# Where two of five weight groups begin inside their buffers in a three-term float32r input projection

## The chip, the cores and the metric

The kernel runs on one core of one Trainium2 chip. The metric is the device time of one execution in microseconds (us). Three runs of the kernel before took 2325.15, 2329.02 and 2332.24 us; their median is 2329.02 us.

## What is computed

One layer of a streaming encoder, for a prompt of 2048 tokens and for 8 sequences of 16 tokens (together 17 tiles of 128 tokens, width 1024). The part that the change touches is the first matrix product:

```python
def trunk_layer(x, ...):
    qm, km, vm, om, ip, fp, qa, ka, va = split_in(x @ w_in)
    ...                                    # mLSTM over chunks, sliding-window attention
    mix = jnp.concatenate([hm, ha], axis=-1) @ w_out
    h = layer_norm(DEEPNORM_ALPHA * x + mix, ln1_g, ln1_b)
    f, conv_rows = conv_ffn(h, conv_prev, w_up, w_conv, b_conv, w_down)
    y = layer_norm(DEEPNORM_ALPHA * h + f, ln2_g, ln2_b)
```

`x @ w_in` is called the in-projection here. It is followed by the output projection (`w_out`), the up-projection (`w_up`, 5632 columns) and the down-projection (`w_down`).

## The kernel before

**Arithmetic.** Every operand of a large product is split into a high part, rounded to float32r by a ScalarE copy, and a low part, the VectorE difference (`split`, lines 218 to 221). A product is then three matmuls: high by high, high by low, low by high.

**In-projection.** The 17 tiles stand in four blocks (`IBLOCKS`): five tiles, then three times four. The columns of `w_in` stand in five groups of 512, `g` = 0 to 4: groups 0 and 1 hold the mLSTM queries and keys, 2 the attention queries, 3 the output gate, 4 the values. Gates and attention keys and values are a sixth, narrower product (`i_direct`, line 760). Each block and group is a 2x2 block product done with seven products instead of eight (`s` = 1 to 7), on sums of quarters. One product (`i_product`, lines 722 to 746) is 24 matmuls at line 735, each with a stationary operand of 128x128 and a moving operand of 128x256: four output quarters, two steps `k`, three terms. The last of the five tiles of block 0 is multiplied apart at line 744.

Which operand is stationary depends on the group:

```python
l, r = (w[:, k, m], x[:, k]) if g < 2 else (x[:, k, m], w[:, k])
mm(o, l, r, ...)
```

In groups 0 and 1 the weights are loaded into the array and the tokens stream past; in groups 2, 3 and 4 it is the other way round. At line 744 the tokens are stationary and the weights move, in every group.

**Where the operands lie.** A weight unit (one product's weights, 1024 float32 in each of 128 partitions, high and low) takes two buffers from `half` (line 396), which hands out the tags `wlo` and `whi` in turn, four buffers each. A buffer is 4608 bytes per partition, since the gate weights (`[P, 2, 2, 288]`, line 485) use the same tags. In the built program the eight buffers begin at 3072, 7680, 12288, 16896, 37888, 42496, 47104 and 51712 bytes into the partition, all multiples of 512. The token operands `oh` and `ol` (`x_slot`, line 543) lie 4096 bytes apart from 65088 on, so each begins 64 bytes after a multiple of 512; that comes from the 256 unused bytes that `self.skew(self.xp, 256)` puts ahead of them (line 246). Within a tile the operands of line 735 begin at multiples of 512 bytes. So before the change the weights begin at 0 and the tokens at 64, counted modulo 512. The token operands of line 744 begin at 384 or 480.

The later projections have other pairs. In the output projection (lines 225 to 227) tokens at 64 are stationary and weights at 0 move, 512 columns at a time. In the up-projection (line 1878; weights stationary, 384 or 320 columns move) and the down-projection (line 2082; tokens stationary, 512 columns move) both operands begin at 0.

**Order.** TensorE's instructions run in the order in which they are written out; the in-projection's products are woven with the chains of the mLSTM and the attention (`Chains.weave`). Weight units are loaded and split ahead as buffers come free (`advance`, `next_raw`, `next_split`). For groups 0 and 1 every weight unit is split by lines 220 and 221 (in blocks 1 to 3 too); only units of groups 2, 3 and 4 are also kept in memory after the split and loaded back by DMA (`kept`, line 425; lines 493 and 533).

Of the kernel before, what the change touches and what calls it, by code (L numbers as in the profile page):

```python
# [14 lines left out]
P = 128  # L15
# [189 lines left out]
class Prog:  # L205
# [269 lines left out]
    def next_split(self):  # L475
        V = self.nc.vector
        if self.us >= self.ur:
            return False
        u = self.uq[self.us]
        need = 1 if u[0] == "g" else 2  # L480
        if self.halves[0] - self.halves[1] + need > self.ring:
            return False
        self.us += 1
        if u[0] == "g":
            e = self.raw_of.pop(u)
            w = self.half([P, 2, 2, 288])[:, :, :, :264]
            self.split(w[:, 0], w[:, 1], e[0])
            e[1] = True
            self.wu[u] = w[:, 0], w[:, 1]
            return True  # L490
        hi, lo = self.half([P, 1024]), self.half([P, 1024])
        if self.kept(u):
            for i, t in enumerate((hi, lo)):
                self.nc.sync.dma_start(t.bitcast(F32), self.zws[u[2]][SUMS.index(u[3])][i].rearrange("p a b -> p (a b)"))
        elif u[0] == "p" and u[1] == 0:
            self.split_first(u[2], u[3], hi, lo)
        else:
            e = self.raw_of.pop(u)
            self.split(hi, lo, e[0].rearrange("p a b -> p (a b)"))
            e[1] = True  # L500
        v = lambda t: t.rearrange("p (a b) -> p a b", a=2 if u[0] == "o" else 4)
        self.wu[u] = v(hi), v(lo)
        return True
# [1670 lines left out]
```

## Time and profile before

| | before |
|---|---|
| median of three runs | 2329.02 us |
| time of the profiled execution | 2327.77 us |
| its span, first to last instruction | 2325.5 us |
| TensorE, matmuls busy | 2292.0 us (99%) |
| TensorE, weight loads busy | 2113.6 us (91%) |
| VectorE busy | 1803.0 us (78%) |
| ScalarE busy | 1305.4 us (56%) |
| mean granted TensorE clock | 0.996 |

The trace gives each matmul a start and a length. The ends are modelled, and the lengths (276 ns and more at line 735) overlap, because the next matmul starts before the one ahead has left the array. So what a stream of matmuls costs is read from the distance of their starts, here called the pace, and not from their length. A row of the timeline merges neighbours of one form: `x2` is two matmuls, and the start shown is that of the first. PE is TensorE's matmuls, PEld its weight loads, DVE VectorE, ACT ScalarE.

### The profile page before, as it was taken

How to read it: one execution, taken by the hardware profiler on the slowest of the kernel's cores; microseconds unless marked ns; L12 is line 12 of the kernel's file. 1: busy time of each engine (PE TensorE's matmuls, PEld its weight loads, DVE VectorE, ACT ScalarE, POOL GpSimd, SP SyncE). 2: the span in 40 equal slices, each digit the busy share in tenths (PEclk: the TensorE clock that was granted, in tenths of full speed). 3: DMA queues.
4: the chain of work that ended last, by engine and by line, in shares of the span. 5: the costliest groups of instructions: out<-in, count | busy, mean ns of one | idle time of the engine just before them, and what ended most of it. 6: DMA issues, size and time to landing. Idle time of an engine off the chain costs nothing.

```text
span 2325.5 us, 39932 instructions
## 1 busy us (share of the span) xinstructions
PE 2292.0 (99%) x14425; PEld 2113.6 (91%) x14425; DVE 1803.0 (78%) x3150; ACT 1305.4 (56%) x2465; POOL 238.0 (10%) x298
## 2 busy tenths in 40 slices
PE   9989999999999999999999999999999999999998
PEld 8989998999987777999999999999999988888887
DVE  8676586787778888987888766778766787796897
ACT  5353466676665665655556455556555644554653
POOL 0101101101111221300002000001000000000100
PEclk9999999999999999999999999999999999999999
DMA  8888889889977667787777899988998886766753
GB/s 281 276 311 283 284 285 315 292 279 341 305 250 262 208 222 242 258 321 286 286 270 251 277 314 327 307 306 268 324 297 265 248 284 224 243 198 215 243 192 109
DMA packets 297365, 624.98 MB, mean 269 GB/s; under 512 B 47052, under 2 KB 140240, under 8 KB 297168
## 3 DMA queue, kind: packets, MB, share of 16 engines
q1 hardware_dynamic: 296304, 619.29, 78.2%
q10 hardware_dynamic: 864, 3.15, 0.4%
q8 instruction: 114, 1.87, 0.3%
q14 instruction: 83, 0.68, 0.1%
HBM read 451.78 MB, written 170.56 MB: 268 GB/s over the span
## 4 chain that ended last, share of the span: by engine, by line
PE 73%; DVE 6%; issue 2%; DMA 2%; ACT 2%; POOL 0%; SPq 0%; DVEq 0%; ACTq 0%; POOLq 0%
PE dps L1878 18%; PE fup L1878 18%; PE dps L2082 6%; PE dps L735 6%; PE fht L2082 5%; PE fup L2082 5%; PE dps L225 2%; PE dps L227 2%; PE dps L226 2%; PE ppo L1371 1%; PE psc L1322 1%; PE ppt L1365 1%; PE dps L760 1%; DVE uw L221 1%; DVE w L221 1%
## 5 line engine op out<-in xcount | busy, mean ns | idle before, releaser
L1878 PE MATMUL dps<-hh,uw 128*128 128x384 f32 (+1 forms) x1848 | 477.5, 327 | 5.3 <-DVE u L1911 2.6
L1878 PE MATMUL fup<-hh,uw 128*128 128x384 f32 (+1 forms) x1848 | 476.4, 326 | 0.0
L1926 DVE SCALAR_TENSOR_TENSOR cc<-u,cw,cc 128x768 f32<-128x768 f32 (+1 forms) x264 | 257.6, 977 | 124.5 <-ACT cc L1924 121.0
L1878 PEld LDWEIGHTS dps<-hh,uw 128*128 128x128 f32 x1848 | 329.2, 188 | 7.6 <-DVE u L1911 3.2
L1878 PEld LDWEIGHTS fup<-hh,uw 128*128 128x128 f32 x1848 | 329.2, 188 | 0.0
L1878 PE MATMUL fup<-hl,uw 128*128 128x384 f32 (+1 forms) x924 | 301.3, 326 | 0.6 <-DVE hl L221 0.6
L1878 PE MATMUL dps<-hl,uw 128*128 128x384 f32 (+1 forms) x924 | 301.0, 326 | 0.0
L735 PE MATMUL dps<-w,oh 128*128 128x256 f32 x1344 | 255.0, 285 | 5.3 <-ACT zev L801 3.6
L221 DVE TENSOR_TENSOR w<-wraw,w 128x1024 fp32r<-128x1024 f32 (+2 forms) x163 | 188.1, 1159 | 60.8 <-ACT w L220 59.5
L220 ACT CAST w<-wraw 128x1024 fp32r<-128x1024 f32 (+2 forms) x163 | 161.0, 993 | 122.0 <-PE dps L735 58.2
L735 PEld LDWEIGHTS dps<-w,oh 128*128 128x128 f32 x1344 | 212.5, 191 | 17.7 <-issue 8.9
L220 ACT CAST uw<-wraw 128x1024 fp32r<-128x1024 f32 x126 | 123.2, 981 | 173.3 <-PE dps L2082 104.1
L221 DVE TENSOR_TENSOR uw<-wraw,uw 128x1024 fp32r<-128x1024 f32 x126 | 142.4, 1130 | 64.0 <-ACT uw L220 63.8
L735 PE MATMUL dps<-w,ol 128*128 128x256 f32 x672 | 188.3, 280 | 0.0
L1924 ACT ACTIVATE cc<-u,cw 128x768 f32<-128x768 f32 (+1 forms) x132 | 132.0, 1000 | 95.3 <-DVE u L1920 92.4
L735 PE MATMUL dps<-oh,w 128*128 128x256 f32 x896 | 171.2, 284 | 5.6 <-ACT zev L801 1.6
L1878 PEld LDWEIGHTS fup<-hl,uw 128*128 128x128 f32 x924 | 173.5, 188 | 1.4 <-DVE hl L221 1.4
L1878 PEld LDWEIGHTS dps<-hl,uw 128*128 128x128 f32 x924 | 173.5, 188 | 0.0
L2082 PE MATMUL fup<-uw,fu 128*128 128x512 f32 x726 | 169.1, 389 | 0.0
L2082 PEld LDWEIGHTS fup<-uw,fu 128*128 128x128 f32 x726 | 136.2, 188 | 28.3 <-ACT fht L2089 0.2
L2082 PE MATMUL dps<-uw,fu 128*128 128x512 f32 x660 | 160.9, 389 | 0.1
L735 PEld LDWEIGHTS dps<-oh,w 128*128 128x128 f32 x896 | 140.8, 188 | 12.3 <-issue 4.1
(337 smaller groups left out, 4612.5 us busy)
## 6 DMA issues: line engine op xcount, KB each, us to landing
uw<-zw SPq DMA_DIRECT2D x176, 512.0 KB, 5.1
zw<-uw SPq DMA_DIRECT2D x88, 512.0 KB, 2.8
w<-zws SPq DMA_DIRECT2D x72, 512.0 KB, 6.6
wv<-wup SPq DMA_DIRECT2D x66, 512.0 KB, 5.9
wraw<-wi SPq DMA_DIRECT2D x64, 512.0 KB, 5.1
wraw<-zt SPq DMA_DIRECT2D x60, 512.0 KB, 4.2
wraw<-wdn SPq DMA_DIRECT2D x45, 512.0 KB, 3.7
wraw<-wo SPq DMA_DIRECT2D x40, 512.0 KB, 4.6
```

What stands on the lines that cost most here:

```text
L220: nc.scalar.copy(hi, src)
L221: nc.vector.tensor_sub(lo, src, hi.bitcast(F32))
L225: mm(out, ah, bh, start=start, stop=False)
L226: mm(out, ah, bl, start=False, stop=False)
L227: mm(out, al, bh, start=False, stop=stop)
L735: mm(o, l, r, start=s in (1, 7) and c == k == i == 0, stop=k == 3 and i == 2, skip_group_check=True)
L760: mm(o, x, w, start=k == i == 0, stop=k == KD - 1 and i == 2, skip_group_check=True)
L1322: nc.tensor.matmul(ps[kvh][:, j, :nk], q[rs, j0 + j], k[rs, sel], start=i == 0, stop=i == 2)
L1878: mm(ps, l[:, k], r[:, k], start=s in (1, 7) and k == 0 and i == 0, stop=k == 3 and i == 2, skip_group_check=True)
L1924: S.activation(c[:, v], u[:, v, 2:2 + n], AF.Identity, bias=w[3], scale=w[2])
L1926: V.scalar_tensor_tensor(c[:, v], u[:, v, i:i + n], w[i], c[:, v], op0=ALU.mult, op1=ALU.add)
L2082: mm(ps, l[:, k, c], r[:, k], start=s in (1, 4, 7) and u == 0 and k == 0 and i == 0, stop=u == nu - 1 and k == n - 1 and i == 2, skip_grou ...
```

## The change

The high and low buffers of a weight unit of groups 0 and 1 (`u[0] == "p" and u[2] < 2`) are taken 128 float32 wider, and the unit's 1024 numbers are put 16 numbers (64 bytes) into them. All other units, those of the output projection among them, stay as they are.

```diff
-        hi, lo = self.half([P, 1024]), self.half([P, 1024])
+        at = 16 if u[0] == "p" and u[2] < 2 else 0
+        hi, lo = [self.half([P, 1024 + 8 * at])[:, at:at + 1024] for _ in range(2)]
```

The wider tile is 4608 bytes, the size that the buffer has already: in the built program every tile begins at the same address as before, and each engine has the same instructions in the same order with the same waits. What differs is the address inside the buffer at which ScalarE and VectorE write the split weights of groups 0 and 1 and at which TensorE reads them. They begin at 64 modulo 512 now, as the tokens do.

## The prediction

> **What bounds the kernel now.** I read the page's head and its busy times first, then the busy time by stage, the groups that use the weight tiles, and the timeline of TensorE in stretches without other work.
>
> ```profile
> span 2325.5 us, 39932 instructions
> PE 2292.0 (99%) x14425; PEld 2113.6 (91%) x14425; DVE 1803.0 (78%) x3150; ACT 1305.4 (56%) x2465; POOL 238.0 (10%) x298
> PE 73%; DVE 6%; issue 2%; DMA 2%; ACT 2%; POOL 0%; SPq 0%; DVEq 0%; ACTq 0%; POOLq 0%
> ```
>
> TensorE has a matmul in flight for 99% of the span, and 73% of the chain that ended last is its own. So nearly every nanosecond that is put between two matmuls should arrive in the total. The stages confirm it where the change lies (span, then PE, PEld, DVE, ACT, POOL busy, granted clock, DMA share, GB/s):
>
> ```profile
> 0.00:70.00 70.00, 64.51 (x505) 62.46 (x506) 58.02 (x104) 37.55 (x60) 0.31 (x5) 1.00 0.83 281
> 70.00:650.00 580.00, 567.69 (x4722) 534.74 (x4722) 414.81 (x1001) 341.56 (x786) 70.79 (x58) 0.99 0.87 297
> ```
>
> From 70 to 650 us TensorE is idle for 12.3 us of 580. In the first 70 us it is idle for 5.5.
>
> **How many matmuls are touched.** The groups of line 735 that read a weight tile, and line 744 beside them:
>
> ```profile
> L735 PE MATMUL dps<-w,oh x1344: 276/276/582, 70.1 to 640.7; 128*128 128x256 f32 x192
> L735 PE MATMUL dps<-oh,w x896: 276/279/471, 6.0 to 552.5; 128*128 128x256 f32 x180
> L735 PE MATMUL dps<-ol,w x448: 276/279/415, 6.2 to 552.4; 128*128 128x256 f32 x150
> L744 PE MATMUL psx<-w,xs x240: 274/280/415, 11.3 to 156.8; 128*128 128x256 f32 x120
> ```
>
> The moving operand's name stands first. Tokens move past weights (`oh,w` and `ol,w`) in 896 + 448 = 1344 matmuls; these are groups 0 and 1, and their stationary operand shifts by 64 bytes. The 2016 with the weights moving (`w,oh`, and `w,ol` in the same proportion) are groups 2 to 4 and keep their addresses.
>
> **What one costs now.** Starts in a clean stretch of group 0 in block 1, weights stationary:
>
> ```profile
> 184.97 0.40 PE L735 MATMUL dps<-oh,w 128*128 128x256 f32 x2
> ...
> 187.79 0.40 PE L735 MATMUL dps<-oh,w 128*128 128x256 f32 x2
> ```
>
> Between these two rows lie 24 matmuls: 2.82 us / 24 = 117.5 ns. The same form in a stretch of group 3, tokens stationary:
>
> ```profile
> 137.77 0.39 PE L735 MATMUL dps<-w,oh 128*128 128x256 f32 x2
> ...
> 140.49 0.39 PE L735 MATMUL dps<-w,oh 128*128 128x256 f32 x2
> ```
>
> 2.72 us / 24 = 113.3 ns. The same size, the same array, the same clock, and 4.2 ns apart; what differs is which operand lies at 0 and which at 64. But the two paces are not tied to the two layouts alone. Once the weights-stationary form ran at the fast pace, and once the other ran at the slow one:
>
> ```profile
> 74.47 0.39 PE L735 MATMUL dps<-oh,w 128*128 128x256 f32 x2
> ...
> 76.51 0.39 PE L735 MATMUL dps<-oh,w 128*128 128x256 f32 x2
> ```
>
> ```profile
> 236.46 0.40 PE L735 MATMUL dps<-w,oh 128*128 128x256 f32 x2
> ...
> 238.94 0.40 PE L735 MATMUL dps<-w,oh 128*128 128x256 f32 x2
> ```
>
> 18 matmuls in 2.04 us are 113.3 ns each; 21 in 2.48 us are 118.1. So a stream falls into one of two steps and keeps it for tens of matmuls. The layout seems to decide which step is the usual one.
>
> **The change part by part.** No instruction, wait or transfer is added, removed or moved, so no queue is passed and no buffer comes free at another point of the program. Two kinds of access change their address.
>
> The writes: 56 units (14 products in 4 blocks) are cast by line 220 and subtracted by line 221, now to a place 64 past a multiple of 512. Token tiles are already written to such places, by lines 580 and 581:
>
> ```profile
> L220 ACT CAST w<-wraw 128x1024 fp32r<-128x1024 f32 x108 | 113.1, 1051 | 94.8 <-PE dps L735 51.6 <-DMA wraw<-wi 12.1 <-PE psx L744 10.8
> L580 ACT CAST oh<-xr 128x1024 fp32r<-128x1024 f32 x23 | 24.0, 1051 | 4.9 <-DVE xr L572 4.3 <-DVE xr L568 0.2 <-DMA xr<-xq 0.2
> L221 DVE TENSOR_TENSOR w<-wraw,w 128x1024 fp32r<-128x1024 f32 x108 | 133.3, 1237 | 49.7 <-ACT w L220 48.6 <-DMA zqa<-zev 0.4 <-DMA wraw<-zws 0.2
> L581 DVE TENSOR_TENSOR ol<-xr,oh 128x1024 fp32r<-128x1024 f32 x23 | 28.5, 1241 | 1.9 <-ACT oh L580 1.9
> ```
>
> 1051 against 1051 ns and 1237 against 1241: the writes cost nothing, and would cost nothing much without cover, since VectorE is busy 414.81 of 580 us there.
>
> The reads: from the pair (stationary 0, moving 64) they go to (64, 64). No 256-column row of the trace has equal places. Wider matmuls with both operands at 0 do: up-projection with 384 and 320 columns, down-projection with 512. The fourth pair is the output projection, 512 columns, stationary at 64 and moving at 0:
>
> ```profile
> 999.71 0.33 PE L1878 MATMUL dps<-hl,uw 128*128 128x384 f32 x1
> ...
> 1001.27 0.33 PE L1878 MATMUL fup<-hl,uw 128*128 128x384 f32 x1
> ```
>
> ```profile
> 1699.94 0.31 PE L1878 MATMUL fup<-hl,uw 128*128 128x320 f32 x1
> ...
> 1700.82 0.31 PE L1878 MATMUL dps<-hl,uw 128*128 128x320 f32 x1
> ```
>
> ```profile
> 2104.82 2.88 PE L2082 MATMUL fht<-uw,fu 128*128 128x512 f32 x12
> 2107.54 0.84 PE L2082 MATMUL dps<-uw,fu 128*128 128x512 f32 x3
> ```
>
> ```profile
> 672.91 0.39 PE L225 MATMUL dps<-w,oh 128*128 128x512 f32 x1
> ...
> 675.01 0.39 PE L225 MATMUL dps<-w,oh 128*128 128x512 f32 x1
> ```
>
> 9 matmuls of 384 columns take 1.56 us, 173.3 each; 6 of 320 take 0.88, 146.7; 12 of 512 take 2.72, 226.7; 9 in the output projection take 2.10, 233.3. The three with equal places lie on one line: 26.6 ns for 64 columns and 53.4 for 128 are both 0.417 ns per column, which leaves 13.3 ns above 320 x 0.417 = 133.4. Carried down to 256 columns that is 106.7 + 13.3 = 120.0 ns. It is an extrapolation: at 256 columns the two known pairs (113.3 and 117.5) lie below the line, so a matmul this short need not behave as the wide ones.
>
> Bounds: at best the shifted form takes the fast step that it has once taken already, 113.3 ns. At worst it pays the line and also what the unequal pair pays at 512 columns, 233.3 - 226.7 = 6.6, so 126.6. I take 120.0, the value from equal places; 117.5 unchanged lies close to it.
>
> Sum: 1344 x (120.0 - 117.5) = +3.4 us. Line 744 moves the shifted weights in 8 of its 20 groups of 12, 96 matmuls, with tokens at 384 or 480; at the 4.2 ns by which the paces differ that is at most 0.4 us either way, taken as 0. Of TensorE's waits in the first 650 us the longest follow its own work:
>
> ```profile
> PE dps L735 <- ACT zev L801: 5.1, 5, 2.3
> PE dps L735 <- ACT zev L793: 2.3, 2, 1.2
> ```
>
> ScalarE copies there what TensorE has just finished, so these 7.4 us move along and absorb nothing. I pass all of the sum on. The profiled execution took 2327.77 us (2.3 around its span); 2327.8 + 3.4 = 2331.2. The median of the runs shown is 1.25 us above that execution, within their spread of 7.1. I name 2331.
>
> **The rivals.** *The fast step* (30%): with the stationary operand at 64, as in groups 2 to 4, the stream settles at 113.3 ns. For it: the stretch at 74.47 us shows that weights-stationary matmuls can run so, and the usual home of that step is a stationary operand at 64. Against it: there the moving operand is at 0, not at 64. It gives 1344 x 4.2 = -5.6 us, 2322.2.
>
> *The address does not matter* (17%): the step is set by how a stream begins, and the usual step of groups 0 and 1 has another cause, such as the order of operands (the stationary one repeated, not the moving one). For it: both paces occur at both layouts. Against it: the split between the groups is too regular for chance. It gives 0, so 2327.8 to 2329. The Trainium skill has this as a rule: "SBUF — State Buffer", section "Who interferes with whom", gives TensorE two independent read ports, one for the moving operand and one for weight loads, and says that it never waits on anyone. By that rule the time stays at 2327.8; the 6.6 ns between the two 512-column streams speak against it here.
>
> *Places count one by one* (13%, the slow side): not the distance of the two operands decides but each start for itself, and a stationary start at 64 costs the 6.6 ns that it seems to cost in the output projection, on top of the line. Then 126.6 ns, 1344 x 9.1 = +12.2 us, 2340. Against it: at 256 columns the stationary start at 64 belongs to the faster group.
>
> My forecast has 38%. The last 2% are other mishaps.
>
> **How the numbers follow.** A measurement of this kernel can tell about 0.3%, 7 us, from no change. The forecast and the no-effect case lie inside that. The fast step lies at 5.6 us, and with some 2 us of scatter in a median it counts as faster in four of ten cases: 0.12, and 0.01 from the rest. Places one by one is slower nearly always, 0.12, and the forecast now and then, 0.03. That leaves 0.72 for the same. The range 2321 to 2337 holds the first three cases but for the lower third of the fast step, and leaves out the slow side: 0.10 + 0.10.
>
> **What would show it.** In the changed profile, the distance of starts in clean stretches of `oh,w`: 120.0 ns if I am right, 113.3, 117.5 or 126.6 for the rivals. Stretches of `w,oh` should stay at 113.3, lines 220 and 221 at 1051 and about 1237 ns, the three wide streams at 146.7, 173.3 and 226.7. I am wrong in kind if the pace is right and the total is not: then idle time has grown or shrunk elsewhere. I am wrong in size if the shifted stream has a third step that no row here shows.

## The result, and the profile after

| | before | after |
|---|---|---|
| median of 12 runs each | 2329.05 us | 2333.47 us |
| lowest to highest | 2325.15 to 2332.24 us | 2327.62 to 2337.48 us |
| profiled execution (its span) | 2327.77 us (2325.5) | 2337.15 us (2334.9) |
| mean granted TensorE clock in it | 0.996 | 0.994 |

The ratio is 1.0019, with a 95% interval of 1.001 to 1.0027: between 2.3 and 6.3 us slower. That is less than the 0.3% that the prediction counts as a change. It lies above the predicted 2331 and inside 2321 to 2337.

The head of the page of the kernel after, its busy times and its chain by engine:

```profile
span 2334.9 us, 39932 instructions
PE 2299.0 (98%) x14425; PEld 2120.2 (91%) x14425; DVE 1802.0 (77%) x3150; ACT 1305.2 (56%) x2465; POOL 245.2 (10%) x298
PE 74%; DVE 6%; issue 3%; DMA 3%; ACT 2%; POOL 0%; SPq 0%; DVEq 0%; POOLq 0%; ACTq 0%
```

The instruction counts are those of before, and TensorE still sets the end. Its busy time has grown by 7.0 us and VectorE's has not. What has changed is in the starts. The groups of the in-projection by operands (line 736 now; shortest, median and longest in ns, then the first and the last start) show where it lies:

```profile
L736 PE MATMUL dps<-oh,w x896: 274/283/470, 6.0 to 560.9; 128*128 128x256 f32 x180
L736 PE MATMUL dps<-w,oh x1344: 276/276/582, 72.1 to 649.6; 128*128 128x256 f32 x192
```

The modelled lengths say little (medians of 283 and 276 ns for 279 and 276), but the last matmul of groups 2 to 4 starts at 649.6 us, where it started at 640.7. So 8.9 of the 9.4 us between the spans arise before 650 us. The pace is in the timeline of a clean stretch of group 0 in block 1, the place shown of before:

```profile
185.64 0.40 PE L736 MATMUL dps<-oh,w 128*128 128x256 f32 x2
...
193.92 0.40 PE L736 MATMUL dps<-oh,w 128*128 128x256 f32 x2
```

69 matmuls in 8.28 us are 120.0 ns each, where it was 117.5 (117.8 over 69 matmuls of the same stretch). The untouched form, tokens stationary, has the pace of before: 63 matmuls in 7.14 us, 113.3 ns.

```profile
106.41 0.39 PE L736 MATMUL dps<-w,oh 128*128 128x256 f32 x2
...
113.55 0.39 PE L736 MATMUL dps<-w,oh 128*128 128x256 f32 x2
```

Nor did a wide stream move: the mean distances of starts of the 320-column, the down-projection's and the output projection's matmuls are 146.7, 226.9 and 233.1 ns in both kernels. In the up-projection 6 matmuls of 384 columns take 1.04 us, 173.3 each:

```profile
1002.56 0.33 PE L1879 MATMUL fup<-hl,uw 128*128 128x384 f32 x1
...
1003.60 0.33 PE L1879 MATMUL dps<-hl,uw 128*128 128x384 f32 x1
```

The writes to the shifted place, by shape (busy us in all, then the mean ns of one), take 1051 ns as before, and 1239 for 1237:

```profile
L220 ACT CAST w<-wraw 128x1024 fp32r<-128x1024 f32 x107 | 112.1, 1051 | 96.6 <-PE dps L736 52.9 <-DMA wraw<-wi 13.7 <-DVE wraw L519 10.9
L221 DVE TENSOR_TENSOR w<-wraw,w 128x1024 fp32r<-128x1024 f32 x107 | 132.3, 1239 | 50.5 <-ACT w L220 50.0
```

The pace accounts for 1344 x 2.5 = 3.4 us, not for the 9.4 us between the two profiled executions. The rest of that is mostly the granted clock of this one execution. Below are three stretches of the kernel before and then of the kernel after (columns as in the prediction: stretch, its length, PE, PEld, DVE, ACT, POOL busy, granted clock, DMA share, GB/s):

```profile
0.00:100.00 100.00, 94.51 (x766) 92.46 (x767) 77.71 (x124) 49.72 (x76) 2.47 (x6) 1.00 0.81 279
100.00:250.00 150.00, 143.30 (x1177) 139.55 (x1178) 102.32 (x158) 64.24 (x95) 22.56 (x16) 0.98 0.85 294
250.00:350.00 100.00, 97.52 (x813) 91.59 (x810) 70.93 (x175) 53.91 (x125) 7.55 (x7) 0.97 0.85 284
```

```profile
0.00:100.00 100.00, 94.31 (x744) 92.45 (x745) 74.24 (x120) 49.84 (x76) 2.47 (x6) 0.98 0.79 272
100.00:250.00 150.00, 141.79 (x1152) 137.97 (x1151) 103.35 (x160) 62.06 (x92) 22.57 (x16) 0.99 0.84 291
250.00:350.00 100.00, 95.93 (x790) 91.02 (x789) 66.06 (x159) 50.51 (x115) 6.57 (x6) 0.92 0.82 270
```

Multiply each stretch by what its clock lacks to 1.00: before loses 0 + 3 + 3 = 6 us, after 2 + 1.5 + 8 = 11.5. The 5.5 us between them and the pace's 3.4 make 8.9 of 9.4. (The clock column is rounded; added up dip by dip from the trace, the losses are 6.8 and 11.9 us.) From 350 to 2320 us both kernels have 1.00. So one execution can't size this change; the medians of 12 can.

### The profile page after: what moved, and what is told of

It reads as the page before. It is cut to its first block, busy times and chain, and to the rows that moved or that the text cites. A ratio compares the mean times of both kernels' runs of the same rounds, so it can differ in the third digit from the quotient of the medians.

```text
span 2334.9 us, 39932 instructions
## 1 busy us (share of the span) xinstructions
PE 2299.0 (98%) x14425; PEld 2120.2 (91%) x14425; DVE 1802.0 (77%) x3150; ACT 1305.2 (56%) x2465; POOL 245.2 (10%) x298
## 4 chain that ended last, share of the span: by engine, by line
PE 74%; DVE 6%; issue 3%; DMA 3%; ACT 2%; POOL 0%; SPq 0%; DVEq 0%; POOLq 0%; ACTq 0%
PE dps L1879 18%; PE fup L1879 18%; PE dps L736 7%; PE dps L2083 6%; PE fht L2083 5%; PE fup L2083 5%; PE dps L225 2%; PE dps L227 2%; PE dps L226 2%; PE ppo L1372 1%; PE psc L1323 1%; PE ppt L1366 1%; PE dps L761 1%; DVE w L221 1%; DMA txy<-wdn 1%
```

## Experiments

The account tested here is that the distance between the starts of the two operands sets the pace. Two others stand beside it: that each place counts for itself, and that the address has no effect. All experiments but the repetitions move operands, and all leave every instruction in its place. Their diffs are against the kernel after, or against the kernel before where its line stands behind the minus; the second line of the first one, the same width for every `at`, belongs to all that set `at` for both halves. Two figures stand for each run: the pace in a clean stretch, and the mean distance of starts over all in-projection matmuls whose successor starts within 160 ns (some 1240 with weights stationary, 1850 with tokens stationary). By that mean before has 117.6 and 114.6, after 119.7 and 114.7. "Distance" is the stationary operand's start minus the moving one's, in bytes: before -64 in groups 0 and 1, after 0. Times are medians, beside those of the kernel before on the same chip.

### Stationary operand 64 bytes past the moving one

```diff
-        at = 16 if u[0] == "p" and u[2] < 2 else 0
-        hi, lo = [self.half([P, 1024 + 8 * at])[:, at:at + 1024] for _ in range(2)]
+        at = 32 if u[0] == "p" and u[2] < 2 else 0
+        hi, lo = [self.half([P, 1152 if at else 1024])[:, at:at + 1024] for _ in range(2)]
```

> Weights of groups 0 and 1 begin 128 bytes in: stationary 128, moving 64. Theory A (the distance of the two starts decides, modulo 512): the distance is +64, as in groups 2 to 4, so the weights-stationary stream falls to 113.3 ns, 1344 x 4.2 = 5.6 us less than before, about 2323. Theory B (each start counts for itself, starts off a multiple of 512 cost): no faster than the 119.7 ns of the changed kernel, 2332 or more. Theory C (addresses have no part): 117.5 ns and the time of before, 2329.

The same units as in the change, 128 bytes into their buffers: the stationary operand at 128, the moving one at 64. The timeline:

```profile
182.30 0.39 PE L736 MATMUL dps<-oh,w 128*128 128x256 f32 x2
...
190.12 0.39 PE L736 MATMUL dps<-oh,w 128*128 128x256 f32 x2
```

69 matmuls in 7.82 us: 113.3 ns, the fast step, now usual in groups 0 and 1 too. The mean fell from 117.6 to 114.8, and 1344 x 2.8 = 3.8 us. Measured: 2326.03 against 2329.64 us, so -3.6 between the medians; the ratio is 0.9988 (0.9978 to 0.9998), a gain of 0.5 to 5.1 us. That is less than the 5.6 expected, since not every stretch ran at 113.3. Another 64 bytes in the same direction turn the loss into a gain, so it is excluded that the address doesn't matter. In the one profiled execution, though, waits took the gain: without what the clock lost up to there, its last in-projection matmul starts at 634.5 us, that of the kernel before at 633.9; the distances of 300 ns and more between starts add up to 52.8 us there, and to 48.8 before.

### A whole period further

```diff
-        at = 16 if u[0] == "p" and u[2] < 2 else 0
+        at = 128 if u[0] == "p" and u[2] < 2 else 0
```

> Weights of groups 0 and 1 begin 512 bytes in, in the same enlarged tile as in the change. Theory A with a period of 512 bytes: the pair is (0, 64) again, 117.5 ns and the time of before, 2329. If the change cost time by the larger tile or by the mere shift, or if the period is longer: another pace, or 2333 as in the changed kernel.

512 bytes on, the pair is (0, 64) again, though the offset inside a wider buffer is the largest tried. The timeline:

```profile
183.21 0.40 PE L736 MATMUL dps<-oh,w 128*128 128x256 f32 x2
...
191.33 0.40 PE L736 MATMUL dps<-oh,w 128*128 128x256 f32 x2
```

69 matmuls in 8.12 us are 117.7 ns each, and the mean is 117.5: the pace of before. The time was 2331.84 against 2329.64 us, ratio 1.0013 (1.0003 to 1.0023), an excess that no pace explains. The same program a second time:

> Weights of groups 0 and 1 begin 512 bytes in, a second time. Its pace was that of before (117.5 ns), its ratio 1.0013. Theory A: 1.000, and the first ratio was scatter between executions (the granted clock). If the larger tile or the shift itself costs time outside the matmul streams: again about 1.001.

2329.01 against 2329.82 us, 0.9994 (0.9983 to 1.0005), with a mean of 117.5 again. The excess of the first time did not come back. Two runs of the same program lie 2.8 us apart in their medians, and their intervals overlap only between 1.0003 and 1.0005. This is the caution for all totals below.

### Distance 0 in all groups

```diff
-        at = 16 if u[0] == "p" and u[2] < 2 else 0
+        at = 16 if u[0] == "p" else 0
```

> Weights of all five groups begin 64 bytes in: the pair is (64, 64) at all of line 735. Theory A: groups 2 to 4 go from 113.3 to 120.0 ns too, 2016 x 6.7 = 13.5 us on top of the 3.4 of groups 0 and 1, about 2346. Theory B with a moving start of 64 as the dear one (it is what groups 0 and 1 have and groups 2 to 4 lack): groups 2 to 4 go to 117.5, 8.5 us on top, about 2341. Theory C: no more than the changed kernel, 2333.

Now the moving weights of groups 2 to 4 begin at 64 as well, beside stationary tokens at 64:

```profile
136.12 0.40 PE L736 MATMUL dps<-w,oh 128*128 128x256 f32 x2
...
144.40 0.40 PE L736 MATMUL dps<-w,oh 128*128 128x256 f32 x2
```

69 in 8.28 us: 120.0 ns, as with the weights stationary. So it isn't the order of the operands, nor whether the stationary one is repeated. The total missed what was expected: 2336.18 against 2329.64 us, ratio 1.0026 (1.0013 to 1.004), +6.5. By the means it should have been 1344 x 2.1 + 2016 x 5.1 = 13.1, beyond the interval's 9.3. The rest is taken up by waits. TensorE's waits for ScalarE in the in-projection:

```profile
PE dps L736 <- ACT zev L794: 2.0, 2, 1.1
...
PE dps L736 <- ACT zev L802: 1.8, 3, 0.8
```

3.8 us together, where before had 7.4. A slower TensorE seems to leave ScalarE time to catch up. Those are two waits among many. Counted by starts, the distances of 300 ns and more in the in-projection (clock dips left out) add up to 42.1 us here, and to between 48.5 and 51.5 in the five profiled executions with the pace of before (before itself 48.8). So some 6 to 9 us of pauses are gone, which is what the total lacks.

### Both operands at 0

```diff
-            self.skew(self.xp, 256)
+            self.skew(self.xp, 192)
-            self.skew(wx, 448)
+            self.skew(wx, 512)
```

> The weights stay at 0 and the tokens move from 64 to 0: the pair is (0, 0) in the in-projection and in the output projection. Theory A: 120.0 ns at all of line 735 (1344 x 2.5 + 2016 x 6.7 = +16.9 us), and the output projection's 512-column stream falls from 233.3 to 226.7 (816 x 6.6 = -5.4 us): about 2340. Theory B: both operands are at the cheap place, so line 735 stays at 113.3 or below in groups 2 to 4 and falls below 117.5 in groups 0 and 1, with the output projection 5.4 us less: 2323 or below. Theory C: 2329.

The kernel before, with the tokens moved back by 64 bytes instead of the weights forward: (0, 0) in all groups, and in the output projection too. The timeline, tokens stationary and then weights stationary:

```profile
136.21 0.40 PE L735 MATMUL dps<-w,oh 128*128 128x256 f32 x2
...
144.49 0.40 PE L735 MATMUL dps<-w,oh 128*128 128x256 f32 x2
...
169.86 0.40 PE L735 MATMUL dps<-oh,w 128*128 128x256 f32 x2
...
177.78 0.40 PE L735 MATMUL dps<-oh,w 128*128 128x256 f32 x2
```

69 in 8.28 and 66 in 7.92 us, 120.0 both. (0, 0) costs what (64, 64) costs, so places do not count one by one. 2335.24 against 2329.64 us, ratio 1.0031 (1.0017 to 1.0046), +5.6, again less than expected. In the output projection, however, 512 columns at distance 0 are cheaper: a mean of 228.8 ns where before has 233.1. 816 matmuls x 4.3 would be 3.5 us, and the sum of the means, 1344 x 2.2 + 2016 x 5.2 - 3.5 = 9.9 us, lies inside the interval (4.0 to 10.7). But the trace shows the parts otherwise. From its first matmul to its last the output projection takes 284.2 us here and 284.4 before: what its stream gains is lost again in longer gaps and in the work woven in. And in the in-projection the pauses of 300 ns and more are 43.2 us, less than in any execution with the pace of before, as in the experiment above.

### Before and after once more

```diff
-        hi, lo = self.half([P, 1024]), self.half([P, 1024])
+        hi = self.half([P, 1024])
+        lo = self.half([P, 1024])
```

> The program of before with the two calls of half written on two lines: the same instructions at the same addresses. Every theory: 117.5 and 114.5 ns, and a ratio to before of 1.000. How far its median and interval lie from that is what a comparison of this size cannot tell.

The program of before, written on two lines: 2329.53 against 2329.82 us, 0.9997 (0.9986 to 1.0008), means 117.4 and 114.6. And the change itself, a second time:

> The changed kernel a second time, beside the program of before. If the pace is the cause (1344 matmuls, 119.7 instead of 117.6 ns), 2.8 to 3.4 us more than before, ratio 1.0012 to 1.0015. If the first 1.0019 also held an effect that the pace does not explain, the ratio stays near 1.002.

The mean is 119.7 again, the stretch 120.0. The time is 2332.49 against 2329.82 us: 2.7 between the medians, while the ratio comes out at 1.0004 (0.9993 to 1.0015), which does not exclude that nothing changed. The pace returns exactly; the total is at the edge of what can be told.

The traces add to this. Take the start of the last in-projection matmul and subtract what the clock lost up to there. In the five profiled executions with the pace of before (before, the one above, the two a whole period further and +192 below) that gives 633.9, 634.7, 634.3, 635.9 and 635.9 us; in the two of the change 637.7 and 638.4. Both lie above all five, by 3.1 us in the mean. This figure scatters too: the executions at +64 (634.5) and -128 (640.9) lie 3 to 4 us above what their paces give.

### The cheapest distance tried for each width

```diff
-        at = 16 if u[0] == "p" and u[2] < 2 else 0
+        at = 16 if u[0] == "o" else 32 if u[2] < 2 else 0
```

> Both distances chosen by theory A: weights of groups 0 and 1 begin 128 bytes in (distance +64, 114.8 instead of 117.6 ns, 1344 x 2.8 = -3.8 us), weights of the output projection 64 bytes in (distance 0, some 228.8 instead of 233.1 ns, 816 x 4.3 = -3.5 us). Together -7.3 us, ratio about 0.997. If the output projection's stream is paced by its waits, only the first part: 0.9985.

+64 in groups 0 and 1, and 0 in the output projection (`"o"`), which had +64. The timeline of the output projection:

```profile
671.05 0.40 PE L225 MATMUL dps<-w,oh 128*128 128x512 f32 x1
...
673.11 0.39 PE L225 MATMUL dps<-w,oh 128*128 128x512 f32 x1
```

9 matmuls in 2.06 us, 228.9 each, against 233.3 before. 2324.67 against 2329.82 us, ratio 0.9976 (0.9966 to 0.9986): a quarter of a per cent below the kernel before, and below the changed kernel too. By the means it should gain 1344 x 2.9 + 816 x 4.7 = 7.7 us; measured is 5.2, with 3.3 to 7.9 in the interval. The second part arrives only by half: from first to last matmul the output projection takes 282.3 us instead of 284.4, so 2.1 of its 3.8 us; longer gaps take the rest.

### The other distances

Three single executions, read for their pace alone:

```diff
-        at = 16 if u[0] == "p" and u[2] < 2 else 0
+        at = 48 if u[0] == "p" and u[2] < 2 else 0     # +128
+        at = 64 if u[0] == "p" and u[2] < 2 else 0     # +192
+        at = 112 if u[0] == "p" and u[2] < 2 else 0    # +384, or -128
```

> Weights of groups 0 and 1 begin 192 bytes in: stationary 192, moving 64, distance +128. One look for the pace. If only distance 0 and those just below it are dear: about 114.8 ns. If +64 alone is cheap: 117 or more.

> Weights of groups 0 and 1 begin 256 bytes in: distance +192. One look for the pace. If only distance 0 and those just below it are dear: about 114.8 ns. If +64 alone is cheap: 117 or more.

> Weights of groups 0 and 1 begin 448 bytes in: distance +384, that is -128 modulo 512. One look for the pace. If what is dear is a weight load that starts just behind the moving stream: 117 or more, like -64 (117.5). If the dear distances end at -64: about 114.8 ns.

The timelines of +128, +192 and +384, in this order:

```profile
182.25 0.40 PE L736 MATMUL dps<-oh,w 128*128 128x256 f32 x2
...
190.44 0.40 PE L736 MATMUL dps<-oh,w 128*128 128x256 f32 x2
```

```profile
183.22 0.40 PE L736 MATMUL dps<-oh,w 128*128 128x256 f32 x2
...
191.34 0.40 PE L736 MATMUL dps<-oh,w 128*128 128x256 f32 x2
```

```profile
185.64 0.40 PE L736 MATMUL dps<-oh,w 128*128 128x256 f32 x2
...
193.83 0.40 PE L736 MATMUL dps<-oh,w 128*128 128x256 f32 x2
```

69 matmuls each, in 8.19, 8.12 and 8.19 us: 118.7, 117.7 and 118.7 ns. +128 is no fast step, so it isn't only distance 0 and the one just below that are dear; of the distances tried, only +64 is fast. +192 has the pace of -64, and +128 that of +384 (-128 counted modulo 512): the two of each pair lie 256 bytes apart and have one pace. No such partner was tried for 0 and for +64. At +128 and -128 the 118.7 is a mean: the starts follow one another in a repeating pattern of about 118, 121, 120, 119 and 115 ns, where distance 0 has 120 each time. The single times, 2335.45, 2332.47 and 2334.34 us beside 2332.24 for one execution of the kernel before, are too few to tell.

### One operand of three

```diff
-        hi, lo = self.half([P, 1024]), self.half([P, 1024])
+        at = 32 if u[0] == "p" and u[2] < 2 else 0
+        hi = self.half([P, 1024])
+        lo = self.half([P, 1152 if at else 1024])[:, at:at + 1024]
```

> Of groups 0 and 1 only the low weights begin 128 bytes in; the high ones stay at 0. In each three matmuls two weight loads come at distance -64 and one at +64. If the pace is set load by load: (2 x 117.6 + 114.8) / 3 = 116.7 ns. If one good or bad load sets the step of the whole stream: 114.8 or 117.6.

Of the three terms of a step, two load the high part (distance -64) and one the low part (+64). Does each load pay for itself, or the stream as a whole? The timeline holds both paces, each for a long time:

```profile
36.35 0.40 PE L737 MATMUL dps<-oh,w 128*128 128x256 f32 x2
...
41.35 0.40 PE L737 MATMUL dps<-oh,w 128*128 128x256 f32 x2
...
179.90 0.39 PE L737 MATMUL dps<-oh,w 128*128 128x256 f32 x2
...
187.72 0.39 PE L737 MATMUL dps<-oh,w 128*128 128x256 f32 x2
```

First 42 in 5.00 us, 119.0 each, then 69 in 7.82, 113.3 each, with the same mixture. The mean over all, 116.7, is that of single loads paying each its own price (two of 117.7 and one of 113.3 make 116.2) only by coincidence: no long stretch runs at it. The 33 unbroken ones of 15 starts or more have means of 113.4 to 114.9 or of 118.5 to 119.2. A third of the loads at +64 was enough to hold a stream in the fast step for 69 matmuls. The one execution took 2325.99 us, too little to set against the run at +64.

## Why the prediction was right

**The pace.** The line through the wide streams with equal places gave 120.0 ns; the shifted stream has 120.0. So the mechanism held, equal places give the line's pace, and not only the number. The doubt that a short matmul need not follow the wide ones is answered for distance 0: there it does, at (64, 64) and at (0, 0), in either order of the operands. The line would have failed at +64, where 256 columns run at 113.3, below the line's 120.0, and 512 columns at 233.3, above 226.7.

**The sum.** +3.4 us was said; +4.4 was measured with an interval of 2.3 to 6.3, and +2.7 between the medians the second time. By the mean of all uninterrupted starts the sum is 1344 x 2.1 = 2.8, since not every stretch ran at its usual pace, and the in-projection of the profiled executions grew by 3.1 us. The 117.5 of the prediction came from rows rounded to 10 ns; the stretch runs at 117.8, which makes the step 2.2 instead of 2.5 and the sum 3.0. The sum is right within what can be measured here; its last microsecond is not shown. It was small enough that a total near 2331 proves little by itself: what carries the account is the pace.

**What costs nothing.** Writes, the untouched form and the 384-column stream stayed as said. Line 744's 96 matmuls were taken as 0; the mean distance at that line is 117.4 ns before and 117.9 and 117.7 in the two executions of the change, 0.1 us over all 240.

**Passing it all on.** "These 7.4 us move along and absorb nothing" held for the change. The two longest waits of the kernel after are

```profile
PE dps L736 <- ACT zev L802: 6.0, 5, 2.9
...
PE dps L736 <- ACT zev L794: 2.6, 1, 2.6
```

8.6 us, no less than before, and 7.6 in the second execution. As a rule it was wrong: with all groups at distance 0 the same waits fell to 3.8 us, and half of the loss was taken up. So the end of those gaps doesn't follow TensorE alone; what else sets it was not tried.

**The rivals.** The *fast step* had the right step and the wrong layout: it belongs to +64, not to a stationary start at 64. *Places one by one* falls with (0, 0) and (64, 64) at one pace. *The address does not matter* falls with paces of 113.3, 117.8 and 120.0 ns in programs that differ in nothing but a start. The prediction took a rule of the Trainium skill for this rival, from "SBUF — State Buffer", section "Who interferes with whom": TensorE's two read ports are independent, and it never waits on anyone. The section is about engines that interfere with each other and does not speak of operand addresses; read as the prediction read it, it would have left all of these paces alike. The measurements differ, and they decide. They don't show where the nanoseconds are spent, in the memory, in the ports or in the array.

**The step that a stream keeps.** The prediction said that the layout decides which step is usual. That is right, and can be said more closely: at distance 0 there is no fast step (weights stationary, 3 of 1236 starts of the kernel after are followed by the next in less than 115 ns, and 57 of 1248 of the kernel before), at +64 it is usual (852 of 1248), at -64 rare (one of the 34 long stretches of the kernel before). Why a stream takes the other step now and then was not tried.

## What to carry to other kernels

Where a kernel loads a new stationary operand for every matmul and TensorE is the bound, read the distance of starts in a clean stretch and compare streams of one shape: here the same 256-column matmul cost 113.3 to 120.0 ns by nothing but the distance between its operands' starts, and distances 256 bytes apart had one pace. Choose that distance for each width by measurement, since the cheapest at 256 columns (+64) is the dearer of the two tried at 512. Then look whether the stage gets shorter too: in the output projection nearly half of the gain was lost in one run and nearly all in another. Trust such a pace from the timeline before a total: with weights stationary its mean came back within 0.2 ns, while medians of one program lay 2.8 us apart.

## What the runs showed of the hardware

The pace at 256 columns, float32r, by distance: 0: 120.0, +64: 113.3, +128 and -128: 118.7, +192 and -64: 117.8 ns (over 69 starts, from the unrounded trace). The period of 256 was not expected: the first experiments counted modulo 512. At 512 columns the two distances that occur stand the other way round: 226.7 to 228.9 at 0 and 233.3 at +64. Steps finer than 64 bytes were not tried.

The granted clock is lost in dips to 0.5 of 3.4 or 6.8 us each, differently in each execution. The same 3.5 us of the kernel before, outside a dip, and of the kernel after, inside one:

```profile
10.40:13.90 3.50, 3.17 (x26) 2.90 (x25) 2.98 (x3) 3.26 (x5) 0.00 (x0) 1.00 1.04 415
10.40:13.90 3.50, 3.50 (x19) 3.50 (x19) 2.69 (x4) 3.25 (x5) 0.00 (x0) 0.51 1.03 411
```

In the dip 256-column starts stand 213 ns apart. Up to 2320 us the dips of before and after lie in the first 350 us; three other executions (both operands at 0, +128, one operand of three) have one at 1590 to 1601 us as well. In the second run of the change the three stretches of above read

```profile
0.00:100.00 100.00, 94.19 (x745) 92.27 (x746) 74.29 (x120) 49.66 (x76) 2.46 (x6) 0.98 0.79 273
100.00:250.00 150.00, 142.71 (x1149) 138.90 (x1148) 103.18 (x159) 62.15 (x92) 22.57 (x16) 0.98 0.84 290
250.00:350.00 100.00, 97.58 (x839) 92.19 (x837) 70.63 (x174) 53.63 (x124) 7.61 (x7) 0.98 0.87 288
```

2 + 3 + 2 = 7 us, with a span of 2330.5 instead of 2334.9 us for the same program: the clock took some 4.5 us less by these rounded columns (5.1 added up dip by dip), and the spans differ by 4.4 us. For these two executions of one program the clock of the first 350 us explains the difference to within a microsecond.
